# End of a decoder layer on TensorE: the rest of a row added by two matmuls, the last quarter squared from PSUM, and weight halves moved by 64 bytes

## The chip, the cores and the metric

One core of a Trainium2 chip runs the kernel. Its engines are TensorE (PE in the profile, with its weight loads as PEld), VectorE (DVE), ScalarE (ACT), GpSimd (POOL) and SyncE (SP, which issues most DMAs). Each engine works through its own queue in order and waits on semaphores for the others. The metric is the device time in microseconds (us); lower is better. For the kernel before it is 483.59 us, the median of three runs (483.5, 483.85 and 483.59).

## The reference

One layer of a hybrid decoder for 256 tokens of width 1024, cut to what matters here:

```
mix = hybrid_mixer(x, ...)                       # mLSTM branch + attention branch, gated, projected
x   = layer_norm(ALPHA * x + mix, ln1_g, ln1_b)
u   = causal_dwconv(x @ w_up, conv_ffn)          # 1024 -> 2 * 2816, three taps along the tokens
g, up = split(u)
ffn = (silu(g) * up) @ w_down                    # 2816 -> 1024
x   = layer_norm(ALPHA * x + ffn, ln2_g, ln2_b)  # mean and variance over the 1024 columns of a token
```

Everything is float32. The kernel keeps that precision by splitting each operand of a product into a high part and a low part of type fp32r and adding three products: high with high, high with low, low with high.

## The kernel before

The weights stream through the core as 81 chunks of 128 rows x 2048 columns (1 MB each); `chunk_order` writes their order out by hand. SP loads a chunk into `raw` five steps ahead; two steps ahead ACT rounds it to the high part `wh` (a CAST) and DVE subtracts to get the low part `wl`. `mm3` issues the three products of one tile. For each chunk a step function (`step_up`, `step_dn`, ...) issues PE's work; `elem_work`, called ahead of it, issues the evacuation of the chunk before and the pieces of the split, in the order of a hand-written list in which `None` stands for the next piece of the split.

The end of the layer. `up` chunks make the hidden features: chunk `up i` gives 128 of them for all 256 tokens; ACT and DVE take them from PSUM (`up_evac`), apply the convolution and the gate, and split the result into `hh` and `hl` (two tiles of 128 x 256; columns 0 to 127 are tokens 0 to 127). `dn` chunks are `w_down`: chunk `dn d` holds the rows for features 2d and 2d+1, each row 1024 columns wide. The last chunks come in the order up 20, up 21, dn 8, dn 9, dn 10, so the three last `dn` chunks (numbers 78, 79 and 80 in the order, with hidden tiles 16 to 21) are worked on together. For up 20 and up 21 and the chunk before them ACT also sums the rows of the weight chunks (`row_sums`), so that a row of the product can give its own mean.

The output is 256 tokens x 1024 columns. Token half 0 accumulates in the PSUM tiles `ffn00` and `ffn01` (columns 0 to 511 and 512 to 1023). Token half 1 has `ffn10`, `ffn11`; for the three last chunks its second 512 columns are dealt with as two quarters, the last 256 columns plus two columns of sums in `ffn11` and columns 512 to 767 in `self.quarter` (`ffn12`). What half 1 had gathered before the last three chunks is added to ALPHA times the input in a tile `r` in SBUF by `so_far`, many microseconds earlier.

PE's order in the last stage is: token half 0 (36 matmuls of 512 columns), token half 1's first 512 columns (18 of 512), then 18 of 258 columns, then 18 of 256 columns into `ffn12`. In `finish`, DVE adds `ffn12` to `r` less the mean (L1201), ACT squares that (L1202), ACT takes the square root of the variance (L1204), DVE the reciprocal (L1205), and three DVE multiplications (L1207) with three stores end the program.

Where the halves of a weight row lie is set by `shift`, `odd` and `col`. In the last three chunks before the change, every 512-column half begins 224 bytes into a stretch of 256 bytes of SBUF (by the addresses in the built program), and so does each `hh` and `hl` tile. In the `up` products the moving operand (`x1h`, `x1l`) begins at 64 of 256 and the stationary weights at 128.

Of the kernel before, what the change touches and what calls it, by code (L numbers as in the profile page):

```python
# [11 lines left out]
F32R = mybir.dt.float32r  # L12
BF16 = mybir.dt.bfloat16
AF = mybir.ActivationFunctionType
ALU = mybir.AluOpType
# [3 lines left out]
P = 128  # L19
S = 256  # L20
D = 1024
# [3 lines left out]
NF = D_FF // P  # L25
# [7 lines left out]
WCOLS = KT * 264 + 64  # L33
# [27 lines left out]
def shift(kind, i):  # L61

    if kind in ("vm", "vb", "o"):
        return 48
    if kind in ("wa", "wb"):
        return 56
    if kind == "dn":

        return 40
    return 0 if kind == "wo" else 16  # L70


class Kernel:
# [27 lines left out]
    def split_parts(self, s):  # L101
        if s >= len(self.order) or s in self.w:
            return []
        raw = self.raw.pop(s)
        if s in self.extra:
            wh, wl = self.extra.pop(s)
            a = 8
        else:
            wh = self.stream.tile([P, WCOLS], F32R, tag="wh", name=f"wh{s}", bufs=3)
            wl = self.stream.tile([P, WCOLS], F32R, tag="wl", name=f"wl{s}", bufs=3)  # L110
            a = shift(*self.order[s])

        e, z, n, _ = odd(*self.order[s])
        last = self.order[s][0] == "dn" and self.order[s][1] >= NF // 2 - 3
        wh, wl = (t[:, a - e:a + 2048 + z + 2 * last] for t in (wh, wl))
        edges = sorted({0, 256 if e else 0, 512 if s == 4 else 0, 2048 if self.order[s][0] == "up" and self.order[s][1] >= 6 else 1024, 2048 - n, 2048})
        cuts = [(*(t[:, self.col(s, b):self.col(s, b) + d - b] for t in (wh, wl)), raw[:, b:d])
                for b, d in zip(edges, edges[1:])]
        self.w[s] = (wh, wl)
        if last:  # L120
            self.summed[self.order[s][1] - (NF // 2 - 3)] = s, raw
        return [lambda c=c: self.split_into(*c) for c in cuts]

    def row_sums(self, n):
# [5 lines left out]

    def split_sums(self, n):
        s, _ = self.summed.pop(n)
        a = self.col(s, D)
        wh, wl = (bass.AP(t.tensor, t.offset + D, [list(t.ap[0]), [a, 2], [1, 2]]) for t in self.w[s])
        self.split_into(wh, wl, self.sums[:, n])

    def col(self, s, c):

        e, z, n, _ = odd(*self.order[s])
        return c + (e if c >= 256 else 0) + (z if c >= 2048 - n else 0)  # L140


# [962 lines left out]
    def step_dn(self, s, d, *a):  # L1105
        nc = self.nc
        if d == 0:
            self.st = [self.ln_tiles(f"2_{t}") for t in range(2)]
            a0 = [self.ps_side([P, 512], f"ffn0{h}") for h in range(2)]
            a1 = [self.ps_side([P, 512], f"ffn1{h}") for h in range(2)]  # L1110
            self.acc = [list(zip(a, ((0, 512), (512, 1024)))) for a in (a0, a1)]
            self.sums = self.fp.tile([P, 3, 2, 2], F32, name="sums")
            nc.gpsimd.memset(self.sums, 0.0)
            self.few = self.fp.tile([P, 8], F32, name="few")

            self.quarter = self.ps_side([P, 256], "ffn12")

        d0 = NF // 2 - 3

        def mm(dd, kk, t, ps, cols, fresh=0):  # L1120
            b = self.col(self.order.index(("dn", dd)), kk * D)
            w = [x[:, b + cols[0]:b + cols[1]] for x in self.w[self.order.index(("dn", dd))]]
            k = 2 * dd + kk
            hh, hl = (x[:, t * P:(t + 1) * P] for x in self.hid[k])
            self.mm3(ps, hh, hl, w[0], w[1], k == fresh, k == (2 * d0 if t and not fresh else NF) - 1)

        def part(t, q):
            ps, cols = self.acc[t][q]
            self.ln_part(self.st[t], self.x1[:, t, :], ps, cols)

        if d < d0:
            for kk in range(2):
                for t in range(2):
                    for ps, cols in self.acc[t]:
                        mm(d, kk, t, ps, cols)
            self.w.pop(s)
            if d == d0 - 1:
                r = self.st[1]["r"]

                def so_far(q):  # L1140
                    ps, cols = self.acc[1][q]
                    c = slice(*cols)
                    nc.vector.scalar_tensor_tensor(r[:, c], self.x1[:, 1, c], ALPHA, ps, op0=ALU.mult, op1=ALU.add)

                def total():
                    nc.scalar.activation(self.st[0]["r"], r, AF.Copy, accum_out=self.few[:, 0:1])
                self.evac[s] = [lambda: so_far(0), lambda: so_far(1), None, total]
            return

        ks = [(d0 + i, kk) for i in range(3) for kk in range(2)]  # L1150
        (p0, c0), (p1, c1) = self.acc[1]
        if d == d0:
            for k in ks:
                for q in self.acc[0]:
                    mm(*k, 0, *q)
            nc.scalar.activation(self.few[:, 7:8], self.mhalf[:, 0:1], AF.Sqrt, scale=-1.0)
            self.evac[s] = [lambda: part(0, 0), lambda: part(0, 1), lambda: self.ln_scale(self.st[0]),
                            lambda: self.ln2_out(0)]
        else:
            if d == d0 + 1:  # L1160
                for k in ks:
                    mm(*k, 1, p0, c0, 2 * d0)

                def add():
                    r = self.st[1]["r"][:, 0:512]
                    nc.vector.tensor_add(r, r, p0)
                self.evac[s] = [add]
            else:
                for k in ks:
                    mm(*k, 1, p1[:, 0:258], (768, D + 2), 2 * d0)  # L1170
                for k in ks:
                    mm(*k, 1, self.quarter, (512, 768), 2 * d0)

    def ln2_out(self, t):
        r = self.st[t]["r"]
# [7 lines left out]
    def finish(self):  # L1183

        nc, v, g, act = self.nc, self.nc.vector, self.nc.gpsimd, self.nc.scalar
        r, c = self.st[1]["r"], self.x1[:, 0, :]
        junk = self.fp.tile([P, 512], F32, name="junk")
        gain, bias = self.lnrow
        total, mean, s0, s1, base, sq, rs = (self.few[:, i:i + 1] for i in range(7))
        ps = self.acc[1][1][0]  # L1190
        lo, mid, hi = slice(0, 512), slice(512, 768), slice(768, D)
        v.tensor_scalar(mean, ps[:, 256:257], total, 1.0 / D, op0=ALU.add, op1=ALU.mult)
        act.activation(junk, r[:, lo], AF.Square, bias=mean, scale=-1.0, accum_out=s0)
        v.scalar_tensor_tensor(r[:, hi], ps[:, 0:256], mean, r[:, hi], op0=ALU.subtract, op1=ALU.add)
        act.activation(junk[:, 0:256], r[:, hi], AF.Square, scale=1.0 / 32.0, accum_out=s1)
        v.scalar_tensor_tensor(c[:, lo], r[:, lo], mean, gain[:, lo], op0=ALU.subtract, op1=ALU.mult)
        g.tensor_scalar(s0, s0, 1.0 / D, EPS, op0=ALU.mult, op1=ALU.add)
        v.tensor_mul(c[:, hi], r[:, hi], gain[:, hi])
        g.tensor_tensor(base, s0, s1, op=ALU.add)

        v.scalar_tensor_tensor(r[:, mid], self.quarter, mean, r[:, mid], op0=ALU.subtract, op1=ALU.add)  # L1201
        act.activation(junk[:, 0:256], r[:, mid], AF.Square, scale=1.0 / 32.0, accum_out=sq)  # L1202
        v.tensor_mul(c[:, mid], r[:, mid], gain[:, mid])
        act.activation(rs, sq, AF.Sqrt, bias=base)  # L1204
        v.reciprocal(rs, rs)  # L1205
        for q in (slice(0, 384), slice(384, 768), hi):
            v.scalar_tensor_tensor(c[:, q], c[:, q], rs, bias[:, q], op0=ALU.mult, op1=ALU.add)  # L1207
            self.store(1, c, q.start, q.stop)
# [7 lines left out]
def odd(kind, i):  # L1216

    if kind == "kb":
        return 0, 8, 128, False
    if kind == "ga" and i < NG - 1:  # L1220
        return 0, 8, 128, True
    if kind == "dn" and i >= NF // 2 - 3:
        return 0, 64, 1024, False
    if (kind, i) == ("up", 2):
        return 0, 8, 256, True
    if (kind, i) in (("up", 0), ("up", 1)):
        return 8, 0, 0, False
    return 0, 0, 0, False
# [14 lines left out]
def _layout(w_in, b_in, conv_qk, mlstm_norm, rel_bias, w_branch_a, w_branch_b, w_out, ln1_g, ln1_b, w_up, conv_ffn,  # L1243
# [22 lines left out]
    def col(a):  # L1266
        return a.reshape(-1, P).T

    vec = np.concatenate(
        [col(b_in[o:o + D]) for o in (O_QM, O_KM, O_QB, O_KB, O_VB, O_GA, O_GB)]  # L1270
        + [col(conv_qk), col(mlstm_norm), col(ln1_g), col(ln1_b), col(conv_ffn)], axis=1)
    rows = np.stack([b_in[O_O:O_O + D], b_in[O_VM:O_VM + D], ln1_g, ln1_b, ln2_g, ln2_b])
    dist = 255 - np.arange(LTOE)
# [33 lines left out]
```

## Time and profile before

| what | before |
|---|---|
| device time, median of 3 | 483.59 us |
| the profiled execution: from first to last instruction | 481.8 us |
| PE, share of the span | 473.9 us, 98% |
| DVE, ACT, POOL | 77%, 62%, 5% |
| mean granted TensorE clock | 0.995 |
| first matmul on the last three chunks | 458.38 us |
| end of the last matmul | 475.15 us |
| from there to the end of the span | 6.65 us |

The profile gives the profiled execution's time as its span; start and end around the span account for the other 1.8 us of the median, and are taken to be equal before and after. Times in the rows are counted from the start of the span. "A <- B" in a row reads "A is written from B". A row with an entry in square brackets had to wait, and the entry names whom for.

### The profile page before, as it was taken

How to read it: one execution, taken by the hardware profiler on the slowest of the kernel's cores; microseconds unless marked ns; L12 is line 12 of the kernel's file. 1: busy time of each engine (PE TensorE's matmuls, PEld its weight loads, DVE VectorE, ACT ScalarE, POOL GpSimd, SP SyncE). 2: the span in 40 equal slices, each digit the busy share in tenths (PEclk: the TensorE clock that was granted, in tenths of full speed). 3: DMA queues.
4: the chain of work that ended last, by engine and by line, in shares of the span. 5: the costliest groups of instructions: out<-in, count | busy, mean ns of one | idle time of the engine just before them, and what ended most of it. 6: DMA issues, size and time to landing. Idle time of an engine off the chain costs nothing.

```text
span 481.8 us, 9426 instructions
## 1 busy us (share of the span) xinstructions
PE 473.9 (98%) x3831; PEld 459.0 (95%) x3831; DVE 370.9 (77%) x666; ACT 298.6 (62%) x509; POOL 22.4 (5%) x42
## 2 busy tenths in 40 slices
PE   8999999999999999999999999999999999999994
PEld 6999999999999999999999999999999999999984
DVE  5798986887688668985677788878668766767886
ACT  6579676685758666966655623766456544655861
POOL 0301002000100010002000001000000000000000
PEclk9999999999999999999999999999999999999998
DMA  7995555464636463643954591727564655455202
GB/s 234 321 325 213 193 188 185 175 222 145 192 136 236 166 192 105 260 177 129 377 195 174 178 346 61 290 88 263 175 209 169 220 190 182 174 210 220 88 1 90
DMA packets 18988, 92.71 MB, mean 192 GB/s; under 512 B 2338, under 2 KB 5614, under 8 KB 9726
## 3 DMA queue, kind: packets, MB, share of 16 engines
q1 hardware_dynamic: 17710, 87.85, 50.8%
q0 software_dynamic: 1232, 4.24, 3.2%
q8 instruction: 30, 0.49, 0.4%
q14 instruction: 16, 0.12, 0.1%
HBM read 91.02 MB, written 1.06 MB: 191 GB/s over the span
## 4 chain that ended last, share of the span: by engine, by line
PE 98%; DVE 0%; ACT 0%; issue 0%; DVEq 0%; ACTq 0%
PE ps_up L148 25%; PE ffn L148 13%; PE ps_ga L148 5%; PE ps_kb L148 5%; PE ps_gb L148 5%; PE ps_qb L148 5%; PE ps_qm L148 5%; PE ps_vm L148 5%; PE mix L148 5%; PE ps_vb L148 5%; PE ps_wb L148 5%; PE ps_wa L148 5%; PE ps_km L148 5%; PE ps_o0b L434 1%; PE ps_o0a L434 1%; PE psn L148 1%
## 5 line engine op out<-in xcount | busy, mean ns | idle before, releaser
L95 DVE TENSOR_TENSOR wl<-raw,wh 128x1024 fp32r<-128x1024 f32 (+4 forms) x147 | 180.0, 1262 | 26.2 <-ACT wh L94 23.5
L94 ACT CAST wh<-raw 128x1024 fp32r<-128x1024 f32 (+4 forms) x147 | 151.9, 1080 | 7.3 <-DMA raw<-in_wst_dram 4.1
L148 PE MATMUL ps_up<-x1h,wl 128*128 128x256 f32 x320 | 88.5, 276 | 0.0
L148 PE MATMUL ps_up<-x1h,wh 128*128 128x256 f32 x320 | 88.4, 276 | 0.0
L148 PE MATMUL ps_up<-x1l,wh 128*128 128x256 f32 x320 | 88.4, 276 | 0.0
L148 PEld LDWEIGHTS ps_up<-x1l,wh 128*128 128x128 f32 x320 | 60.1, 188 | 0.4
L148 PEld LDWEIGHTS ps_up<-x1h,wh 128*128 128x128 f32 x320 | 60.1, 188 | 0.3
L148 PEld LDWEIGHTS ps_up<-x1h,wl 128*128 128x128 f32 x320 | 60.1, 188 | 0.0
L1085 DVE SCALAR_TENSOR_TENSOR cu<-ps_up,vec,cu 128x255 f32<-128x255 f32 (+1 forms) x80 | 33.1, 476 | 20.4 <-ACT cu L1081 20.4
L148 PE MATMUL ffn<-wh,hl 128*128 128x512 f32 (+2 forms) x94 | 35.5, 378 | 0.0
L148 PE MATMUL ffn<-wl,hh 128*128 128x512 f32 (+2 forms) x94 | 35.5, 377 | 0.0
L148 PE MATMUL ffn<-wh,hh 128*128 128x512 f32 (+2 forms) x94 | 35.3, 375 | 0.0
L94 ACT CAST hh<-cu 128x256 fp32r<-128x256 f32 x22 | 8.9, 406 | 40.4 <-DVE cu L1096 40.4
L1081 ACT ACTIVATE cu<-ps_up,vec 128x256 f32<-128x256 f32 x40 | 16.7, 469 | 22.5 <-PE ps_up L148 22.5
L148 PEld LDWEIGHTS ffn<-wh,hl 128*128 128x128 f32 x94 | 17.7, 188 | 3.2
L148 PEld LDWEIGHTS ffn<-wl,hh 128*128 128x128 f32 x94 | 17.7, 188 | 3.1
L148 PEld LDWEIGHTS ffn<-wh,hh 128*128 128x128 f32 x94 | 17.7, 188 | 3.0
L148 PE MATMUL ps_ga<-xth,wh 128*128 128x256 f32 x64 | 18.0, 281 | 0.0
L148 PE MATMUL ps_qm<-xth,wh 128*128 128x256 f32 x64 | 17.9, 280 | 0.0
L148 PE MATMUL mix<-wh,mgh 128*128 128x256 f32 x64 | 17.8, 279 | 0.0
L148 PE MATMUL ps_qb<-xth,wh 128*128 128x256 f32 x64 | 17.8, 278 | 0.0
L148 PE MATMUL ps_gb<-xth,wh 128*128 128x256 f32 x64 | 17.8, 278 | 0.0
(340 smaller groups left out, 1445.0 us busy)
## 6 DMA issues: line engine op xcount, KB each, us to landing
raw<-in_wst_dram SPq DMA_DIRECT2D x72, 1024.0 KB, 4.9
raw<-in_wst_dram SPq DMA_DIRECT2D x10, 512.0 KB, 6.7
raw<-in_wst_dram SPq DMA_DIRECT2D x8, 256.0 KB, 4.5
lnrow<-in_rows_dram POOLq DMA_DIRECT2D x4, 512.0 KB, 6.7
xraw<-in_xt_dram SPq DMA_DIRECT2D x8, 128.0 KB, 2.8
toe<-table POOLq DMA_DIRECT2D x4, 256.0 KB, 5.3
xtok<-in_x_dram POOLq DMA_DIRECT2D x1, 1024.0 KB, 8.1
sgb<-in_wst_dram SPq DMA_DIRECT2D x4, 128.0 KB, 3.5
```

Of the source, the lines that this page charges most:

```text
L94: self.nc.scalar.copy(wh, raw)
L95: self.nc.vector.tensor_sub(wl, raw, wh.bitcast(F32))
L148: self.nc.tensor.matmul(ps, a[i], b[i], start=start and i == 0, stop=stop and i == 2)
L434: mm(ps[t], x[:, k, t * P:(t + 1) * P], w, start=start and k == 0, stop=stop and k == KT - 1)
L1081: act.activation(cu[:, j, :], ps[:, j, :], AF.Copy, scale=tap(2, j))
L1085: v.scalar_tensor_tensor(cu[:, j, o:], ps[:, j, :S - o], tap(t, j), cu[:, j, o:], op0=ALU.mult, op1=ALU.add)
```

## The change

Three things are edited.

1. In the three last `dn` chunks the second halves of the two rows lie elsewhere in `wh` and `wl`: they now begin 160 bytes into a stretch of 256 bytes, 64 lower than before; the first halves stay at 224. A split's piece is still one row of 1024 columns, but it is now written as two runs of 512.
2. Token half 0's second 512 columns are worked on as two pieces of 256. The loops are turned for that: all 18 matmuls of the first 512 columns come first, over all three chunks, then 36 matmuls of 256 columns.
3. The rest of the row (columns 512 to 767 of `r`) is split into high and low parts (`res`) after step dn 7, and two matmuls with an identity (`unit`) add it to `ffn12` ahead of the last quarter. `finish` then has ACT square `ffn12` out of PSUM, with the mean as a bias, and DVE apply the gain to `ffn12` directly; the two DVE instructions L1201 and L1203 become one (L1226), and a one-column multiplication (L1221) is new.

The diff, cut to its core (line numbers after it are higher by 13 to 23 than before):

```diff
     def split_parts(self, s):
...
+        if last:
+            wh, wl = (t[:, 0:WCOLS] for t in (wh, wl))
...
+            def halves(t, k):
+                b, c = self.col(s, k * D), self.col(s, k * D + 512)
+                return bass.AP(t.tensor, t.offset + b, [list(t.ap[0]), [c - b, 2], [1, 512]])
...
     def col(self, s, c):
+        if kind == "dn" and i >= NF // 2 - 3:
+            k, c = divmod(c, D)
+            return ((552, 1064) if c < 512 else (24 - 512, 1624 - 512))[k] + c
...
     def step_dn(self, s, d, *a):
...
+                def keep():
+                    nc.scalar.copy(self.unit, self.ident)
+                    self.split_into(*self.res, r[:, 512:768])
+                self.evac[s] = [lambda: so_far(0), lambda: so_far(1), None, total, keep]
...
         if d == d0:
+            (a0, b0), (a1, _) = self.acc[0]
             for k in ks:
-                for q in self.acc[0]:
-                    mm(*k, 0, *q)
+                mm(*k, 0, a0, b0)
+            for k in ks:
+                for j in range(2):
+                    mm(*k, 0, a1[:, j * 256:(j + 1) * 256], (512 + j * 256, 768 + j * 256), open=j == 0)
...
                 for k in ks:
                     mm(*k, 1, p1[:, 0:258], (768, D + 2), 2 * d0)
+                for i, h in enumerate(self.res):
+                    nc.tensor.matmul(self.quarter, self.unit, h, start=i == 0, stop=False)
                 for k in ks:
-                    mm(*k, 1, self.quarter, (512, 768), 2 * d0)
+                    mm(*k, 1, self.quarter, (512, 768), 2 * d0, True)
...
     def finish(self):
...
+        v.tensor_scalar(part, mean, 1.0 / 32.0, None, op0=ALU.mult)
         v.tensor_mul(c[:, hi], r[:, hi], gain[:, hi])
...
-        v.scalar_tensor_tensor(r[:, mid], self.quarter, mean, r[:, mid], op0=ALU.subtract, op1=ALU.add)
-        act.activation(junk[:, 0:256], r[:, mid], AF.Square, scale=1.0 / 32.0, accum_out=sq)
-        v.tensor_mul(c[:, mid], r[:, mid], gain[:, mid])
+        act.activation(junk[:, 0:256], self.quarter, AF.Square, bias=part, scale=-1.0 / 32.0, accum_out=sq)
+        v.scalar_tensor_tensor(c[:, mid], self.quarter, mean, gain[:, mid], op0=ALU.subtract, op1=ALU.mult)
```

What it does to the order of the instructions, at three places. In the rows a name's number tells the buffers of one kind apart: `hh18` is the hidden tile 18, `wh79` the high part of chunk 79.

PE before, the 13th to 18th matmul of the last stage (the first one stands just behind the last matmul of up 21): they work on hidden tile 18 and chunk 79, once for each half of the columns.

```order
L148 MATMUL ffn00_4129<-wh79_5539,hh18_5410 128x512
L148 MATMUL ffn00_4129<-wl79_5540,hh18_5410 128x512
L148 MATMUL ffn00_4129<-wh79_5539,hl18_5411 128x512
L148 MATMUL ffn01_4130<-wh79_5539,hh18_5410 128x512
L148 MATMUL ffn01_4130<-wl79_5540,hh18_5410 128x512
L148 MATMUL ffn01_4130<-wh79_5539,hl18_5411 128x512
```

PE after, the 13th to 20th matmul of the same stage.

```order
L161 MATMUL ffn00_4129<-wh80_5617,hh20_5558 128x512
L161 MATMUL ffn00_4129<-wl80_5618,hh20_5558 128x512
L161 MATMUL ffn00_4129<-wh80_5617,hl20_5559 128x512
L161 MATMUL ffn00_4129<-wh80_5617,hh21_5630 128x512
L161 MATMUL ffn00_4129<-wl80_5618,hh21_5630 128x512
L161 MATMUL ffn00_4129<-wh80_5617,hl21_5631 128x512
L161 MATMUL ffn01_4130<-wh78_5473,hh16_5244 128x256
L161 MATMUL ffn01_4130<-wl78_5474,hh16_5244 128x256
```

Chunk 80 and the hidden tiles 20 and 21 have moved up: the first use of `wl80` from the 26th matmul to the 14th, that of `hh21` from the 31st to the 16th, that of `hl21` from the 33rd to the 18th. What makes them, on ACT and DVE, has not moved.

ACT before, from the gate of up 21 to the end of the program:

```order
L1081 ACTIVATE cu_5613<-ps_up_5562,vec 128x256 x2
L94 CAST wh_5611<-raw_5416 128x1024 x2
L1092 ACTIVATE cu_5613<-cu_5613 128x256
L128 ACTIVATE r_0_4121,sums<-raw_5416 128x1024 x2
L94 CAST hh_5624<-cu_5613 128x256
L94 CAST wh_5611<-sums 128x2x2
L1156 ACT_TABLE_LOAD
L1156 ACTIVATE few<-mhalf 128x1
L1193 ACTIVATE junk,few<-r_1_4125,few 128x512
L1195 ACTIVATE junk,few<-r_1_4125 128x256
L1202 ACTIVATE junk,few<-r_1_4125 128x256
L1204 ACTIVATE few<-few 128x1
```

ACT after, the same place:

```order
L1094 ACTIVATE cu_5619<-ps_up_5568,vec 128x256 x2
L94 CAST wh_5617<-raw_5422 128x2x512 x2
L1105 ACTIVATE cu_5619<-cu_5619 128x256
L136 ACTIVATE r_0_4121,sums<-raw_5422 128x1024 x2
L94 CAST hh_5630<-cu_5619 128x256
L94 CAST wh_5617<-sums 128x2x2
L1177 ACT_TABLE_LOAD
L1177 ACTIVATE few<-mhalf 128x1
L1216 ACTIVATE junk,few<-r_1_4125,few 128x512
L1218 ACTIVATE junk,few<-r_1_4125 128x256
L1225 ACTIVATE junk,few<-ffn_4139,few 128x256
L1227 ACTIVATE few<-few 128x1
```

The order is the same: two casts of chunk 80 and two sums of its rows stand ahead of the cast of hidden tile 21. The casts write two runs of 512 each, and the last square reads `ffn12` (here `ffn_4139`).

DVE at the end, before:

```order
L1198 TENSOR_TENSOR x_3016<-r_1_4125,lnrow_4303 128x256
L1201 SCALAR_TENSOR_TENSOR r_1_4125<-ffn_4136,few,r_1_4125 128x256
L1203 TENSOR_TENSOR x_3016<-r_1_4125,lnrow_4303 128x256
L1205 RECIPROCAL few<-few 128x1
L1207 SCALAR_TENSOR_TENSOR x_3016<-x_3016,few,lnrow_4305 128x384 x2
L1207 SCALAR_TENSOR_TENSOR x_3016<-x_3016,few,lnrow_4305 128x256
```

And after:

```order
L1221 TENSOR_SCALAR few<-few 128x1
L1222 TENSOR_TENSOR x_3016<-r_1_4125,lnrow_4306 128x256
L1226 SCALAR_TENSOR_TENSOR x_3016<-ffn_4139,few,lnrow_4306 128x256
L1228 RECIPROCAL few<-few 128x1
L1230 SCALAR_TENSOR_TENSOR x_3016<-x_3016,few,lnrow_4308 128x384 x2
L1230 SCALAR_TENSOR_TENSOR x_3016<-x_3016,few,lnrow_4308 128x256
```

One instruction fewer stands between the last matmul and the reciprocal; L1226 waits for ACT's square (L1225), where L1201 waited for PE. The orders of SP and POOL are the same in both kernels.

More of the change, by code (lines that the diff above doesn't have):

```diff
@@ L114, in split_parts @@
         last = self.order[s][0] == "dn" and self.order[s][1] >= NF // 2 - 3
-        wh, wl = (t[:, a - e:a + 2048 + z + 2 * last] for t in (wh, wl))
+        if last:
+            wh, wl = (t[:, 0:WCOLS] for t in (wh, wl))
+            self.w[s] = (wh, wl)
+            self.summed[self.order[s][1] - (NF // 2 - 3)] = s, raw
+            def halves(t, k):
+                b, c = self.col(s, k * D), self.col(s, k * D + 512)
+                return bass.AP(t.tensor, t.offset + b, [list(t.ap[0]), [c - b, 2], [1, 512]])
+            return [lambda k=k: self.split_into(halves(wh, k), halves(wl, k), raw[:, k * D:(k + 1) * D].rearrange(
+                "p (a b) -> p a b", a=2)) for k in range(2)]
+        wh, wl = (t[:, a - e:a + 2048 + z] for t in (wh, wl))
         edges = sorted({0, 256 if e else 0, 512 if s == 4 else 0, 2048 if self.order[s][0] == "up" and self.order[s][1] >= 6 else 1024, 2048 - n, 2048})
@@ L119, in split_parts @@
         self.w[s] = (wh, wl)
-        if last:
-            self.summed[self.order[s][1] - (NF // 2 - 3)] = s, raw
         return [lambda c=c: self.split_into(*c) for c in cuts]
@@ L132, in split_sums @@
         s, _ = self.summed.pop(n)
-        a = self.col(s, D)
-        wh, wl = (bass.AP(t.tensor, t.offset + D, [list(t.ap[0]), [a, 2], [1, 2]]) for t in self.w[s])
+        a, b = (self.col(s, k * D + 512) + 512 for k in range(2))
+        wh, wl = (bass.AP(t.tensor, t.offset + a, [list(t.ap[0]), [b - a, 2], [1, 2]]) for t in self.w[s])
         self.split_into(wh, wl, self.sums[:, n])
     def col(self, s, c):
-        e, z, n, _ = odd(*self.order[s])
+        kind, i = self.order[s]
+        if kind == "dn" and i >= NF // 2 - 3:
+            k, c = divmod(c, D)
+            return ((552, 1064) if c < 512 else (24 - 512, 1624 - 512))[k] + c
+        e, z, n, _ = odd(kind, i)
         return c + (e if c >= 256 else 0) + (z if c >= 2048 - n else 0)
@@ L1114, in step_dn, with mm @@
             self.few = self.fp.tile([P, 8], F32, name="few")
+            self.unit = self.fp.tile([P, P], F32R, name="unit")
+            self.res = [self.fp.tile([P, 256], F32R, name=f"res{n}") for n in "hl"]
             self.quarter = self.ps_side([P, 256], "ffn12")
         d0 = NF // 2 - 3
-        def mm(dd, kk, t, ps, cols, fresh=0):
-            b = self.col(self.order.index(("dn", dd)), kk * D)
-            w = [x[:, b + cols[0]:b + cols[1]] for x in self.w[self.order.index(("dn", dd))]]
+        def mm(dd, kk, t, ps, cols, fresh=0, more=False, open=False):
+            b = self.col(self.order.index(("dn", dd)), kk * D + cols[0])
+            w = [x[:, b:b + cols[1] - cols[0]] for x in self.w[self.order.index(("dn", dd))]]
             k = 2 * dd + kk
             hh, hl = (x[:, t * P:(t + 1) * P] for x in self.hid[k])
-            self.mm3(ps, hh, hl, w[0], w[1], k == fresh, k == (2 * d0 if t and not fresh else NF) - 1)
+            self.mm3(ps, hh, hl, w[0], w[1], k == fresh and not more, k == (2 * d0 if t and not fresh else NF) - 1 and not open)
         def part(t, q):
@@ L1146, in total @@
                     nc.scalar.activation(self.st[0]["r"], r, AF.Copy, accum_out=self.few[:, 0:1])
-                self.evac[s] = [lambda: so_far(0), lambda: so_far(1), None, total]
+                def keep():
+                    nc.scalar.copy(self.unit, self.ident)
+                    self.split_into(*self.res, r[:, 512:768])
+                self.evac[s] = [lambda: so_far(0), lambda: so_far(1), None, total, keep]
             return
@@ L1188, in finish @@
         gain, bias = self.lnrow
-        total, mean, s0, s1, base, sq, rs = (self.few[:, i:i + 1] for i in range(7))
+        total, mean, s0, s1, base, sq, rs, part = (self.few[:, i:i + 1] for i in range(8))
         ps = self.acc[1][1][0]
@@ L1221, in odd @@
         return 0, 8, 128, True
-    if kind == "dn" and i >= NF // 2 - 3:
-        return 0, 64, 1024, False
     if (kind, i) == ("up", 2):
```

## The prediction

> **What bounds the kernel now.** I read the page's chain first, then the end of the chain of waits, then the rows of ACT, DVE and PE in the last stage.
>
> ```profile
> PE 473.9 (98%) x3831; PEld 459.0 (95%) x3831; DVE 370.9 (77%) x666; ACT 298.6 (62%) x509; POOL 22.4 (5%) x42
> ```
>
> PE is busy for 98% of the span, so the time is PE's matmuls plus what stands behind the last one. The chain of waits from 454.9 us (start, length, what):
>
> ```profile
> 454.91 3.63 PE ps_up L148 x32
> 458.55 16.61 PE ffn L148 x90
> 475.15 0.03 issue
> 475.18 0.49 DVE r L1201
> ...
> 475.71 0.34 issue
> 476.05 0.52 ACT junk L1202 x2
> ...
> 476.65 0.30 ACT few L1204
> ...
> 476.98 0.17 DVE few L1205
> ```
>
> PE runs through the last stage without a gap, and 1.83 us pass from its end (475.15) to the reciprocal (476.98). The change works on both. So I ask first whether PE still has its operands in time. ACT and DVE in that stage (start, length):
>
> ```profile
> 459.03 0.83 ACT L1081 ACTIVATE cu<-ps_up,vec 128x256 f32<-128x256 f32 x2
> 459.75 1.99 ACT L94 CAST wh<-raw 128x1024 fp32r<-128x1024 f32 x2
> 461.96 1.05 ACT L128 ACTIVATE r<-raw 128x1024 f32<-128x1024 f32 x1
> 463.13 1.06 ACT L128 ACTIVATE r<-raw 128x1024 f32<-128x1024 f32 x1
> 464.19 0.40 ACT L94 CAST hh<-cu 128x256 fp32r<-128x256 f32 x1
> ...
> 461.46 2.35 DVE L95 TENSOR_TENSOR wl<-raw,wh 128x1024 fp32r<-128x1024 f32 x2
> 463.73 0.42 DVE L1096 TENSOR_TENSOR cu<-cu 128x256 f32<-128x256 f32 x1
> 464.62 0.43 DVE L95 TENSOR_TENSOR hl<-cu,hh 128x256 fp32r<-128x256 f32 x1 [0.47 <-ACT hh L94]
> ```
>
> These make chunk 80 and hidden tile 21. The first row of `wl80` is done at about 462.65 (half of 2.35 behind 461.46), `hh21` at 464.59, `hl21` at 465.05. PE's 1st, 13th, 14th, 19th, 31st and 33rd matmul of the stage:
>
> ```profile
> 458.38 0.39 PE L148 MATMUL ffn<-wh,hh 128*128 128x512 f32 x1
> ...
> 461.14 0.39 PE L148 MATMUL ffn<-wh,hh 128*128 128x512 f32 x1
> 461.37 0.39 PE L148 MATMUL ffn<-wl,hh 128*128 128x512 f32 x1
> ...
> 462.50 0.39 PE L148 MATMUL ffn<-wh,hh 128*128 128x512 f32 x1
> ...
> 465.23 0.39 PE L148 MATMUL ffn<-wh,hh 128*128 128x512 f32 x1
> ...
> 465.68 0.39 PE L148 MATMUL ffn<-wh,hl 128*128 128x512 f32 x1
> ```
>
> One per 0.227 us (4.54 us for 20). Before, the 31st is the first to use `hh21` and starts 0.64 us after it is there; the 33rd has 0.63 us to spare for `hl21`. That is all the slack there is.
>
> **The turned loops.** By the order, `wl80` is now wanted by the 14th matmul, `hh21` by the 16th and `hl21` by the 18th, while their makers stay where they are: up 21 ends on PE at 458.5 as before, and ACT is full from then to the cast of `hh21`. What a weight load costs that PE could not take ahead shows at 82.5 us, where one waited:
>
> ```profile
> 82.52 0.19 PEld L822 LDWEIGHTS pso<-pth,vbh 128*128 128x128 f32 x1
> 82.55 0.36 PE L822 MATMUL pso<-pth,vbh 128*128 128x256 f32 x1
> ...
> 82.75 0.38 PE L823 MATMUL pso<-ptf,vbf 128*128 128x128 f32 x2
> ```
>
> A 256-column matmul is followed after 0.20 us there instead of 0.11, so 0.09 a time. Then: 14th due at 461.37, waits for 462.65, starts at about 462.73; 15th at 463.05 (0.227 + 0.09); 16th due at 463.28, waits for 464.59, starts at 464.65; 17th at 464.97; 18th at 465.20, when `hl21` is just there; the next begins at 465.43. Before, the 19th begins at 462.50. The first wait is 1.3 us, the second 1.3 to 1.4, and the stage stands **2.93 us later**. Nothing covers it: PE's queue is in order, and the 36 quarter matmuls that could run meanwhile are queued behind the waiting ones. Bounds: without any cost of loads 2.75, with a third exposed load 3.05.
>
> **The pieces of 256 and the 64 bytes.** The rate of a 256-column matmul differs by place:
>
> ```profile
> 470.67 0.28 PE L148 MATMUL ffn<-wh,hh 128*128 128x258 f32 x1
> ...
> 472.82 0.28 PE L148 MATMUL ffn<-wh,hh 128*128 128x256 f32 x1
> ...
> 474.86 0.28 PE L148 MATMUL ffn<-wh,hl 128*128 128x256 f32 x1
> ```
>
> The 18 of 258 columns take 2.15 us (0.119 each) and the last 18 follow each other in 0.120, while `ps_up` in the chain does 32 in 3.63, 0.1134 each. In `ps_up` the weights loaded next lie 64 bytes further on (modulo 256) than the moving operand; in the last stage both lie at 224. The change makes it 160 and 224, the same 64, so I take 0.1134 (0.1143 for 258 columns). Then token half 0's 36 pieces cost 4.08 us against 18 x 0.227 = 4.09: nothing. The 18 of 258 gain 0.09, the last 17 spacings 0.11. If 0.120 stays: 0, 0 and +0.24 for the pieces, so 0.44 worse together. [...] This trace has both rates side by side, so I go by the rows.
>
> **The two added matmuls.** `res` and `unit` lie both at 64 of 256, a distance that no fast group has: 0.12 each, **+0.24** (bounds 0.23 at the fast rate, 0.41 with both loads exposed). Their making, in `keep`, is two ACT casts of at most 0.41 us and one DVE subtraction of 0.43, after step dn 7. The cover is there:
>
> ```profile
> 442.25 0.84 ACT L1081 ACTIVATE cu<-ps_up,vec 128x256 f32<-128x256 f32 x2 [2.15 <-PE ps_up L148]
> ...
> 443.13 1.66 DVE L1085 SCALAR_TENSOR_TENSOR cu<-ps_up,vec,cu 128x255 f32<-128x255 f32 x4 [1.74 <-ACT cu L1081]
> ```
>
> ACT sat idle 2.15 us and DVE 1.74 before the evacuation that follows, so it costs nothing; without that cover at most 0.8 us, and up 18's gate would be late for dn 9, ten microseconds on. The casts and subtractions in two runs of 512 have no row of their own; I take the 1024 row, give 0.1 us either way, and it enters through `wl80` and `hh21`.
>
> PE's end: +2.93 - 0.09 + 0.24 - 0.11 = **+2.97**, at about 478.1.
>
> **Token half 0's normalisation** is DVE's work beside PE:
>
> ```profile
> 467.44 0.67 DVE L975 SCALAR_TENSOR_TENSOR r<-x,ffn 128x512 f32<-128x512 f32 x1
> ...
> 472.51 0.68 DVE L1166 TENSOR_TENSOR r<-r,ffn 128x512 f32<-128x512 f32 x1
> ```
>
> From its second half to the end of L1166 it needs 5.75 us. `ffn01` is now done at about 469.7, so DVE is free at 475.5; the mean (L1215) is due when the 258-column matmuls end, at about 475.8. Hidden by 0.3 us; if that goes, the excess is added only as far as it passes the 2.3 us of PE behind it.
>
> **The tail.** Before: 1.83 us from PE's end to the reciprocal. After: ACT waits for PE in the semaphore instruction that held L1202 back, so I keep the 0.34 us of issue seen ahead of it: the square starts 0.39 after PE's end. It took 0.52 from SBUF; from PSUM I add 0.05:
>
> ```profile
> L1081 ACT ACTIVATE cu<-ps_up,vec 128x256 f32<-128x256 f32 x40 | 16.7, 469 | 22.5 <-PE ps_up L148 22.5
> ```
>
> (469 ns for 256 columns from PSUM against 0.42 from SBUF), so it ends at 0.96. L1226 may not touch `ffn12` before that: 0.98 to 1.47 (0.49 as L1201). The root ends at 1.35. The reciprocal follows at 1.47 instead of 1.83: **-0.36**. If the 0.34 of issue is not met again, -0.70; if the square is no shorter and DVE starts late, -0.2. Behind the reciprocal nothing changes.
>
> **The sum:** +2.97 - 0.36 = +2.61 on a span of 481.8, 484.4; the median is 1.8 above the span, so 483.59 + 2.61 = **486.2 us** (+0.54%). With the ends of every term together: 485.5 to 486.9.
>
> **Rivals.**
> A. *The clock falls during the waits.* Rows of the granted clock (PEclk ahead of the DMA share) behind PE's end:
>
> ```profile
> 476.00:477.00 1.00, 0.00 (x0) 0.00 (x0) 0.14 (x2) 0.80 (x3) 0.00 (x0) 1.00 0.03 8
> 477.00:478.00 1.00, 0.00 (x0) 0.00 (x0) 0.96 (x3) 0.00 (x0) 0.00 (x0) 0.53 0.00 0
> ```
>
> It fell to 0.5 at 477.06, after 1.9 us without a matmul. The two waits together are 2.7 us with 0.5 us of matmuls between. Against it: neither alone is 1.9. How long the half rate would last is bounded from above by the start of the kernel:
>
> ```profile
> 1.25 3.60 PE L202 MATMUL warm_ps<-warm 128*128 128x512 bf16 x8 [1.25 <-DVE warm L199]
> ...
> 6.09 0.28 PE L434 MATMUL ps_o3b<-wh,xth 128*128 128x264 f32 x1
> ```
>
> Full rate came 4.8 us after the first matmul, so a fall costs 0 to 2.4 us; I take 1.5: 487.7. [...]
>
> B. *The 64 bytes do nothing* (the change doesn't do what it says): 486.2 + 0.44 = 486.6.
>
> C. *No slower: the wait is short.* If the two-run casts and subtractions of chunk 80 ran much faster, `hh21` would come earlier. Without any wait the rest sums to -0.09 + 0.24 - 0.11 - 0.36 = -0.32: 483.3. For the time to stay within 0.2% (0.97 us, about what a measurement of this kernel can tell from no change) the delay must fall from 2.93 to under 1.29, so chunk 80's casts (1.99 us) would have to shrink to some 0.35 and the subtractions (2.35) likewise. For it speaks only that no row shows the two-run form; against it, that the number of elements is the same.
>
> **Chances.** The forecast 0.57, A 0.28, B 0.08, C 0.05, something else that makes it faster 0.02. The likeliest is 486.2. The range reaches from the low end of the forecast, 485.5, over B to 488.0, which leaves out the dear end of A: about 0.15 lies outside. Slower by over 0.2%: 0.93; within: 0.05; faster: 0.02, since without any wait the tail alone gives 0.3 to 0.7 us.
>
> **What would show it.** In the trace after: two gaps on PE at 461.4 to 462.7 and 463.3 to 464.6, the second ended by ACT's `hh` cast; `ffn` matmuls of 256 columns at 0.1134; PE's last end near 478.1; L1225 0.39 us after it, the reciprocal 1.47 after it; granted clock 1.0 until then, or 0.5 in a row near 464 to 468 (A). I am wrong if PE shows no gap there, or if it takes the pieces of 256 columns first.

## The result, and the profile after

The changed kernel takes **487.75 us**, the median of six runs (485.82, 487.62, 487.68, 487.82, 487.91, 490.05), against 483.74 for the kernel before in six runs beside it: a ratio of **1.0081 (95% interval 1.0069 to 1.0094)**. It is slower, as forecast, and 1.55 us slower than the likeliest case said. Four of the six stand within 0.3 us of each other, at the 487.7 of rival A. Of 21 executions of the kernel before beside the first four experiments one took 975.13 us; the ratios there leave it out.

The profiled execution took 487.62 with a span of 485.9 us, 4.1 more than before. First line 1 of the page, then the timeline of PE at the start of the last stage (start, length, and in brackets the idle time ahead and what ended it).

```profile
PE 475.9 (98%) x3851; PEld 460.8 (95%) x3851; DVE 370.5 (76%) x667; ACT 299.1 (62%) x511; POOL 22.4 (5%) x42
```

```profile
458.51 0.39 PE L161 MATMUL ffn<-wh,hh 128*128 128x512 f32 x1
...
461.27 0.39 PE L161 MATMUL ffn<-wh,hh 128*128 128x512 f32 x1
462.86 0.50 PE L161 MATMUL ffn<-wl,hh 128*128 128x512 f32 x1 [1.20 <-DVE wl L95]
463.20 0.40 PE L161 MATMUL ffn<-wh,hl 128*128 128x512 f32 x1
464.76 0.50 PE L161 MATMUL ffn<-wh,hh 128*128 128x512 f32 x1 [1.17 <-ACT hh L94]
...
465.56 0.28 PE L161 MATMUL ffn<-wh,hh 128*128 128x256 f32 x1
```

The two gaps are where the prediction put them, and the tiles it named end them. PE's share of the span still reads 98%: 2.4 us of idle time do not show in a share. What follows shows in the table by stretches. Its columns are the stretch, its length, the busy time of PE, PEld, DVE, ACT and POOL with their instructions, then the granted clock, the DMA share and GB/s.

```profile
458.89:462.31 3.42, 2.77 (x13) 1.91 (x11) 2.79 (x7) 3.42 (x8) 0.00 (x0) 1.00 0.00 0
462.31:465.72 3.41, 1.69 (x7) 1.05 (x8) 2.46 (x5) 3.36 (x7) 0.00 (x0) 1.00 0.00 0
465.72:469.13 3.41, 3.41 (x19) 3.41 (x18) 1.38 (x2) 0.59 (x2) 0.00 (x0) 0.50 0.02 5
...
465.56:471.28 5.72, 5.72 (x38) 5.71 (x36) 1.38 (x2) 0.75 (x2) 0.00 (x0) 0.70 0.01 3
471.28:475.37 4.09, 4.09 (x20) 3.38 (x19) 3.72 (x9) 0.00 (x0) 0.68 (x1) 1.00 0.01 2
475.37:477.55 2.18, 2.18 (x19) 2.17 (x18) 1.88 (x5) 0.00 (x0) 0.00 (x0) 1.00 0.33 126
```

From 465.72 to 469.13 the clock is 0.50. PE is full there and does half the work: 256-column matmuls follow each other every 0.213 us, instead of 0.11 behind 469.22. The 36 pieces take the 5.72 us of the fourth row, where 18 matmuls of 512 columns take 4.09 (18 x 0.227). The end, from the chain of waits:

```profile
464.76 12.95 PE ffn L161 x75
477.71 0.23 PE ffn L1193 x2
477.95 2.05 PE ffn L161 x18
480.00 0.03 ACTq L1225
480.03 0.05 issue
480.07 0.57 ACT junk L1225 x2
...
480.67 0.48 DVE x L1226
481.16 0.08 DVE few L1228
...
481.26 0.62 DVE x L1230
```

Before, the first of the last multiplications stood here in the chain:

```profile
477.17 0.62 DVE x L1207
```

From PE's end to it, it is 1.26 us now (480.00 to 481.26); before it was 2.02 (475.15 to 477.17). So PE's end is 4.85 us later, and the tail gives 0.76 back: 4.1 us of span.

### The profile page after: what moved, and what is told of

It reads as the page before. It is cut to its first block, busy times and chain, and to the rows that moved or that the text cites. A ratio compares the mean times of both kernels' runs of the same rounds, so it can differ in the third digit from the quotient of the medians.

```text
span 485.9 us, 9470 instructions
## 1 busy us (share of the span) xinstructions
PE 475.9 (98%) x3851; PEld 460.8 (95%) x3851; DVE 370.5 (76%) x667; ACT 299.1 (62%) x511; POOL 22.4 (5%) x42
## 4 chain that ended last, share of the span: by engine, by line
PE 93%; ACT 4%; issue 1%; DMA 1%; DVE 0%; SPq 0%; DVEq 0%; ACTq 0%
PE ps_up L161 21%; PE ffn L161 12%; PE ps_ga L161 5%; PE ps_kb L161 4%; PE ps_gb L161 4%; PE ps_qb L161 4%; PE ps_qm L161 4%; PE ps_vm L161 4%; PE mix L161 4%; PE ps_vb L161 4%; PE ps_wb L161 4%; PE ps_wa L161 4%; PE ps_km L161 4%; ACT wh L94 1%; ACT r L136 1%; PE ps_o0a L447 1%
## 5 line engine op out<-in xcount | busy, mean ns | idle before, releaser
L161 PE MATMUL ffn<-wl,hh 128*128 128x512 f32 (+2 forms) x100 | 37.3, 373 | 1.2 <-DVE wl L95 1.2
L161 PE MATMUL ffn<-wh,hh 128*128 128x512 f32 (+2 forms) x100 | 37.0, 370 | 1.2 <-ACT hh L94 1.2
L161 PE MATMUL ffn<-wh,hl 128*128 128x512 f32 (+2 forms) x100 | 37.2, 372 | 0.0
L161 PEld LDWEIGHTS ffn<-wh,hh 128*128 128x128 f32 x100 | 19.6, 196 | 4.3 <-ACT hh L94 1.6
L161 PEld LDWEIGHTS ffn<-wl,hh 128*128 128x128 f32 x100 | 19.5, 195 | 4.4 <-DVE wl L95 1.6
L161 PEld LDWEIGHTS ffn<-wh,hl 128*128 128x128 f32 x100 | 19.6, 196 | 3.1 <-DVE hl L95 0.2
```

What stands on the lines that cost most here:

```text
L161: self.nc.tensor.matmul(ps, a[i], b[i], start=start and i == 0, stop=stop and i == 2)
```

## The experiments

Times are medians of runs beside the kernel before, in about the order in which they were run. Each heading names the kernel that the edit is against; "ratio" is always to the kernel before.

**The turned loops turned back** (against the changed kernel; eleven runs). The split layout, the pieces, the added matmuls and the new tail stay; only the order over rows is that of before.

```
                 mm(*k, 0, a0, b0)
-            for k in ks:
                 for j in range(2):
```

> The changed kernel with one thing undone: token half 0 goes chunk row by chunk row again (first 512 columns, then the two pieces of 256, then the next row), so that chunk 80 and hidden tile 21 are wanted late, as before. Theory W (the turned loops make PE wait, and the waits make the clock fall): no gap on PE over 0.3 us in the last stage, granted clock 1.0 until PE's end, and what is left of the change counts: tail -0.76 (1.07 us from PE's end to the reciprocal, as the changed kernel's trace has it, against 1.83), the two added matmuls +0.24, the last 18 matmuls at 0.1134 -0.11, 258 columns +0.02: -0.6 us against before, about 483.1. Rival P (the pieces of 256 or the moved halves themselves slow PE or bring the clock down): still slower than before by 1.5 us or more, with the half rate somewhere in the pieces.

Measured: 483.31 against 483.75, ratio **0.9988 (0.9979 to 0.9997)**. No gap on PE, clock 1.00 up to PE's end. Its end, from the chain of waits:

```profile
473.64 2.05 PE ffn L161 x18
475.70 0.03 ACTq L1224
475.73 0.05 issue
475.77 0.57 ACT junk L1224 x2
...
476.37 0.48 DVE x L1225
...
476.96 0.62 DVE x L1229
```

The tail is 1.26 us, as in the changed kernel. All of the loss is the order of the loops; what is left of the change is a gain of some 0.4 us. It is a little smaller than the tail's 0.76 because PE's stage (from its first matmul to its last end) is 17.04 us instead of 16.75.

**Idle matmuls in both waits** (against the changed kernel; four runs). Six matmuls of 512 columns into an unused PSUM tile stand ahead of each row of chunk 80, so that PE has work while it would wait.

```
             for k in ks:
+                if k[0] == d0 + 2:
+                    filler(6)
                 mm(*k, 0, a0, b0)
```

> The changed kernel with matmuls of no use in the waits: ahead of each of chunk 80's two rows in the turned loop six 512-column matmuls of ready operands go into a PSUM tile that nobody reads (1.36 us each time, about the length of the wait). Theory W with the clock as a second step: chunk 80's operands come no earlier, so the last matmul ends as late as in the changed kernel without a fall of the clock (its one run without one was 485.82), granted clock 1.0 through the stage: 485.8 to 486.1. Rival (the clock does not follow PE's idleness, or the 1.7 us has another cause, such as the pieces of 256): 487.6 or more, the 256-column matmuls at 0.21 us for some 3.4 us as in the changed kernel.

Measured: 486.22 (485.84 to 486.32), ratio 1.0045 (1.003 to 1.006), clock 1.00 up to PE's end. From the chain of waits:

```profile
461.45 1.36 PE idle L1178 x6
462.81 0.79 PE ffn L161 x3
463.60 1.38 PE idle L1178 x6
```

The two waits are still there, as 2.74 us of idle matmuls, and the stage takes 20.04 us: 3.00 more than with the loops turned back. Without the gaps' effect on the clock the time is 1.5 us below the changed kernel's, and it is the prediction's likeliest case, 486.2, to the tenth. That close an agreement is luck: the stage is 3.29 us longer than before where +2.97 was forecast, and the tail 0.76 shorter where 0.36 was. So the loss has two parts: 2.9 to 3.0 us of waits and about 1.5 us of clock.

**The turned loops alone** (against the kernel before; four runs). One matmul for the second 512 columns, old layout, old tail.

```
-            for k in ks:
-                for q in self.acc[0]:
+            for q in self.acc[0]:
+                for k in ks:
                     mm(*k, 0, *q)
```

> The kernel before with only the two loops of token half 0 turned: all 18 matmuls of its first 512 columns, then 18 of 512 columns for the second; halves, tail and last quarter as before. Theory W: both waits are there (1.2 to 1.4 us each at the 14th and 16th matmul), +2.8 us, and the clock falls in most runs, +1.7: 486.5 where it doesn't fall, 488.2 where it does, median near 488. Rival P: the loops alone cost little, under 1 us, 483.7 to 484.7.

Measured: 487.49 (486.67 to 488.41), ratio 1.0074 (1.0059 to 1.0088). PE, and the end in the chain of waits:

```profile
463.00 0.50 PE L148 MATMUL ffn<-wl,hh 128*128 128x512 f32 x1 [1.20 <-DVE wl L95]
...
464.91 0.50 PE L148 MATMUL ffn<-wh,hh 128*128 128x512 f32 x1 [1.17 <-ACT hh L94]
```

```profile
480.57 0.32 issue
480.89 0.52 ACT junk L1202 x2
```

The same two gaps, the same half clock behind them (0.50 from 465.72 to 469.13 in this execution), the stage 4.59 us longer than before. In the stretch ahead of the fall PE was busy for 1.55 us:

```profile
462.30:465.72 3.42, 1.55 (x6) 0.90 (x7) 2.62 (x5) 3.37 (x8) 0.00 (x0) 1.00 0.00 0
```

The pieces of 256 columns and their layout have no part in the loss. The median is no higher than the changed kernel's although the old tail is 0.76 us longer; the four executions lie 1.7 us apart (486.67, 487.02, 487.97, 488.41), so the clock probably did not cost the same in each; only the slowest of them has a trace.

**The tail alone** (against the kernel before; eleven runs). `res`, `unit`, their two matmuls and the new lines of `finish`; loops and layout as before.

```
+                for i, h in enumerate(self.res):
+                    nc.tensor.matmul(self.quarter, self.unit, h, start=i == 0, stop=False)
                 for k in ks:
-                    mm(*k, 1, self.quarter, (512, 768), 2 * d0)
+                    mm(*k, 1, self.quarter, (512, 768), 2 * d0, True)
...
-        act.activation(junk[:, 0:256], r[:, mid], AF.Square, scale=1.0 / 32.0, accum_out=sq)
+        act.activation(junk[:, 0:256], self.quarter, AF.Square, bias=part, scale=-1.0 / 32.0, accum_out=sq)
```

> The kernel before with only the tail of the change: the rest of the row added by two matmuls with the identity, ACT squares the last quarter from PSUM; halves and loops as before. If the tail is worth what the changed kernel's trace shows (1.07 us instead of 1.83 from PE's end to the reciprocal) and the two matmuls cost 0.24: -0.5 us, about 483.2. If the 0.34 us of issue ahead of the square comes back: 1.4 to 1.5 us and -0.15. If splitting the rest of the row delays the up stage: no gain, 483.7 or more.

Measured: 483.32 (482.96 to 483.71), ratio **0.9988 (0.998 to 0.9997)**. From the chain of waits:

```profile
473.11 0.23 PE ffn L1177 x2
473.34 2.16 PE ffn L148 x18
475.50 0.03 ACTq L1209
475.53 0.05 issue
475.57 0.57 ACT junk L1209 x2
```

The whole gain comes from this part. The last 18 matmuls take 2.16 us here and 2.05 where their operand lies 64 bytes lower.

**The second half in one matmul** (against the first experiment; eleven runs): no pieces of 256 columns for token half 0.

```
-                for j in range(2):
-                    mm(*k, 0, a1[:, j * 256:(j + 1) * 256], (512 + j * 256, 768 + j * 256), open=j == 0)
+                mm(*k, 0, a1, b1)
```

> The first experiment's kernel (loops interleaved, halves moved, new tail) with token half 0's second 512 columns worked on in one matmul again instead of two pieces of 256. In the first experiment the pieces cost 0.1175 us each, 4.23 us for 36, where 18 matmuls of 512 columns at 0.227 cost 4.09. If a 512-column matmul from the moved halves keeps 0.227: 0.15 us less than the first experiment, 483.15. If the moved halves suit 256 columns only, and 512 go at 0.233 to 0.237 as some rows at the start of the stage: within 0.05 us of it, 483.3.

Measured: 483.58 (483.13 to 484.36) against 483.91, ratio 0.9994 (0.9985 to 1.0003). The stage is 17.07 us, with the pieces 17.04. One matmul of 512 or two of 256 make no difference that can be seen here.

**The square's bias from a tile** (against the kernel before; one run). The issue time ahead of the square had shrunk from 0.34 to 0.05 us, which the prediction had only as a bound of its sum. The changed kernel's square has a bias column; here the old square gets one, of zeros.

```
-        act.activation(junk[:, 0:256], r[:, mid], AF.Square, scale=1.0 / 32.0, accum_out=sq)
+        act.activation(junk[:, 0:256], r[:, mid], AF.Square, bias=self.zero[:, 0:1], scale=1.0 / 32.0, accum_out=sq)
```

> The kernel before; the last square (L1202) is given a bias column of zeros from a tile, as the changed kernel's square has a bias column. It tells why 0.34 us of issue stood ahead of the square before and 0.05 in the changed kernel. If the bias from a tile is the difference: about 0.05 us from the release to the square, and some 0.3 us less from PE's end to the reciprocal. If not (what runs beside it on DVE, or where it reads): 0.32 to 0.34 again.

Measured: 484.13 against 483.91. From the chain of waits:

```profile
476.20 0.34 issue
476.54 0.61 ACT junk L1204 x2
```

The 0.34 us stay; the bias is not their reason.

**Other distances** (against the first experiment; one run). The second halves of chunk 78, of chunk 79 and of chunk 80's two rows lie 96, 160, 32 and 0 bytes below the next weights (modulo 256), where the change has 64 for all.

```
-            return ((552, 1064) if c < 512 else (24 - 512, 1624 - 512))[k] + c
+            off = {0: (-8, -8), 1: (-24, -24), 2: (8, 16)}[i - (NF // 2 - 3)][k]
+            return ((552, 1064) if c < 512 else (24 - 512 + off, 1624 - 512 + off))[k] + c
```

> The first experiment's kernel with the second halves of the last three chunks' rows at other places: the weights loaded next (the hidden tiles, at 224 of 256 bytes) lie 96 bytes further on than the moving operand for chunk 78, 160 for chunk 79, 32 for the first row of chunk 80 and 0 for its second, instead of 64 for all. One look at the spacing of the last 18 matmuls (256 columns), six or three for each distance. If the distance sets the rate and 64 is its best: 0.120 at 0, as before the change, and more than 0.1134 at the others. If any place but the old one is as good: 0.1134 at 32, 96 and 160. If the place is not what matters: 0.1134 throughout.

Measured: 483.63 against 483.91. The last 18 matmuls, which go through all three chunks, from the chain of waits:

```profile
473.84 2.15 PE ffn L162 x18
```

At the four places together they take 2.15 us (0.118 to 0.119 from one to the next on the mean of each place), where at 64 bytes it was 2.05 in the first experiment (0.1133). With all at 0 bytes, in the tail alone, it was 2.16. So the place did act on these 18, and of the five distances only 64 did it. The edit moves the halves and the distance together, so it does not tell these two apart; in `ps_up`, where the halves lie elsewhere at the same 64 bytes, the rate is 0.1134 too.

**Idle matmuls in the first wait only** (against the changed kernel; four runs): the filler of the second experiment, only where the first row of chunk 80 begins.

```
+                if k == (d0 + 2, 0):
+                    filler(6)
                 mm(*k, 0, a0, b0)
```

> The changed kernel with matmuls of no use in the first of the two waits alone (six of 512 columns, 1.36 us), so that one wait of some 1.2 to 1.5 us is left at the 16th matmul. Theory: the clock falls when a window of some 3.4 us is idle for more than half; one wait is too short for that: granted clock 1.0 through the stage and 486.0 to 486.3 in every run, as with both waits filled. Rival: any wait over a microsecond can bring it down: some runs at 487.6 to 487.9.

Measured: 486.31 (486.17 to 486.52), ratio 1.005 (1.0036 to 1.0064). By stretches of 3.41 us:

```profile
462.36:465.77 3.41, 2.23 (x10) 1.31 (x9) 2.74 (x5) 3.36 (x8) 0.00 (x0) 1.00 0.00 0
465.77:469.18 3.41, 3.41 (x30) 3.37 (x29) 1.38 (x2) 0.87 (x2) 0.00 (x0) 1.00 0.02 5
```

One wait of 1.2 us alone leaves the clock at 1.00, at nearly the same place in time as in the changed kernel; it takes both. That points to a count over a stretch rather than to the length of a gap. Rows of the kernel before and of the one with the bias tile, behind PE's end, say how much is enough:

```profile
473.65:477.06 3.41, 1.49 (x13) 1.28 (x11) 2.18 (x6) 1.83 (x7) 0.47 (x2) 1.00 0.17 64
477.06:480.47 3.41, 0.00 (x0) 0.00 (x0) 1.62 (x4) 0.00 (x0) 0.00 (x0) 0.50 0.43 154
```

```profile
473.90:477.31 3.41, 1.70 (x15) 1.50 (x13) 2.31 (x5) 1.93 (x7) 0.47 (x2) 1.00 0.22 82
477.31:480.72 3.41, 0.00 (x0) 0.00 (x0) 1.71 (x4) 0.22 (x1) 0.00 (x0) 1.00 0.42 151
```

The stretches are laid back from where the clock changed. Behind 1.49 us of PE work it was halved; behind 1.70 it stayed, and fell one stretch later. With 1.69 in the changed kernel it fell. In the kernel before the trace has the clock full from 6.02 to 477.06, 138 times 3.413 us; in the changed kernel it was full from 4.92 to 465.72, 135 times, half to 469.13, once, and full to 482.79, four times. The border, between 1.69 and 1.70 us, is at about half of a stretch. On such stretches all thirteen profiles agree. Of those at full clock, nine with 0.04 to 1.69 us of PE work and six with none were each followed by the half clock, and none with 1.70 or more was.

**Two idle matmuls in each wait** (against the changed kernel; four runs) tests that border: PE idles some 0.7 us twice and keeps over half of any stretch.

```
+                if k[0] == d0 + 2:
+                    filler(2)
                 mm(*k, 0, a0, b0)
```

> The changed kernel with two idle matmuls of 512 columns (0.227 us each) ahead of each row of chunk 80 in the turned loop, where the earlier run had six. The waits still end when wl80 and hh21 are there, so PE's work behind them stays 2.9 us late. Theory 1: the clock is judged over windows of 3.41 us, and is halved behind a window in which PE was busy for no more than half (1.69 us and less in the windows seen so far; 1.70 and more left it at full). The two waits leave PE some 2.4 us without work in the changed kernel, and 1.5 us here, so every window of 3.41 us keeps at least 1.9 us of work wherever it lies: the clock stays at 1.0, and every execution takes 485.8 to 486.5 us. Theory 2: any pair of waits of about 0.8 us close together brings the clock down: 487.7 in most executions, as for the changed kernel. Theory 3: only the length of a single gap counts, and 1.3 us is just over it in some executions; here the gaps are 0.8 us, and it gives the same as theory 1.

Measured: 485.84 (485.59 to 486.21), ratio 1.0047 (1.003 to 1.0063), clock 1.00:

```profile
462.51:465.93 3.42, 2.73 (x14) 1.98 (x15) 2.42 (x5) 3.33 (x8) 0.00 (x0) 1.00 0.00 0
465.93:469.34 3.41, 3.41 (x32) 3.41 (x31) 0.79 (x2) 0.00 (x0) 0.00 (x0) 1.00 0.02 5
```

Two gaps of 0.75 and 0.69 us (ahead of the matmuls at 462.43 and 464.34) did not bring the clock down, so it isn't pairs of waits as such. It fits the border at half and does not prove it: by this experiment alone the length of the gaps could count too. But one gap of 1.2 us left the clock alone in the experiment before, and two brought it down, which the length of a gap does not explain.

**The gain's multiplication later** (against the kernel before; one run): DVE's second reading of `r` is moved away from the square.

```
-        v.tensor_mul(c[:, mid], r[:, mid], gain[:, mid])
         act.activation(rs, sq, AF.Sqrt, bias=base)
         v.reciprocal(rs, rs)
+        v.tensor_mul(c[:, mid], r[:, mid], gain[:, mid])
```

> The kernel before, with DVE's multiplication of the last quarter by the gain (L1203), which reads the same r as ACT's square, moved behind the reciprocal. In the kernel before ACT's square stands 0.34 us of issue behind the instruction that waited for DVE; in the changed kernel it stands 0.05 us behind. A bias column taken from a tile, as the changed kernel has one, left the 0.34 as it was. Theory 1: a second reader of r starting on DVE at the same moment held the square back; then it follows after about 0.05 us here, and the reciprocal comes 0.3 us sooner behind PE's end (1.5 us instead of 1.83). Theory 2: the 0.34 us belongs to being released by DVE's write instead of by PE; then it stays at 0.32 to 0.34 us. The time moves by less than 0.4 us either way: 483.4 to 484.2.

Measured: 483.71 against 483.70. From the chain of waits:

```profile
475.67 0.34 issue
476.01 0.52 ACT junk L1202 x2
```

**The square from PSUM, still behind DVE** (against the kernel before; one run): L1201 writes back into `ffn12`.

```
-        v.scalar_tensor_tensor(r[:, mid], self.quarter, mean, r[:, mid], op0=ALU.subtract, op1=ALU.add)
-        act.activation(junk[:, 0:256], r[:, mid], AF.Square, scale=1.0 / 32.0, accum_out=sq)
-        v.tensor_mul(c[:, mid], r[:, mid], gain[:, mid])
+        v.scalar_tensor_tensor(self.quarter, self.quarter, mean, r[:, mid], op0=ALU.subtract, op1=ALU.add)
+        act.activation(junk[:, 0:256], self.quarter, AF.Square, scale=1.0 / 32.0, accum_out=sq)
+        v.tensor_mul(c[:, mid], self.quarter, gain[:, mid])
```

> The kernel before, with L1201 writing its result back into ffn12 in PSUM instead of into r in SBUF; ACT squares it and DVE multiplies it by the gain from there. The release of the square still comes from DVE, but the source is PSUM, as in the changed kernel. The 0.34 us of issue ahead of the square stood as they were with a bias from a tile, and with the multiplication moved away. Theory 1: they come with a release by DVE; then they stay at 0.32 to 0.34. Theory 2: they come with a source in SBUF that was just written; then the square follows after 0.05 here, as in the changed kernel. Time by theory 1 483.3 to 484.1, by theory 2 some 0.2 less.

Measured: 483.84 against 483.85.

```profile
476.03 0.34 issue
476.37 0.48 ACT junk L1202 x2
```

Neither the bias nor a second reader nor the memory of the source is the reason of the 0.34 us. Two differences are left: the engine that releases the square (PE instead of DVE), and that ACT's semaphore instruction ahead of it then waits for two engines and ends with PE (479.24 to 480.03 in the changed kernel). Neither is the reason by itself, by rows of the kernel before. There ACT's first square is released by DVE too, and it starts 0.03 us behind DVE's end (473.33); its wait is its own, without a semaphore instruction ahead:

```profile
473.11 0.22 DVE L1192 TENSOR_SCALAR few<-ffn,few 128x1 f32<-128x1 f32 x1
473.36 0.72 ACT L1193 ACTIVATE junk<-r,few 128x512 f32<-128x512 f32 x1 [7.15 <-DVE few L1192]
```

And the root (L1204), whose semaphore instruction waits for one engine alone, ACT itself, stands 0.04 us of issue behind it (476.60). What remains possible is a semaphore instruction released by DVE; no run shows it apart from this one square.

## Why the prediction was right or wrong

The direction and the mechanism of the waits were right, and the time lies in the range given, which had been drawn up to 488.0 to take in most of rival A. The likeliest case, 485.5 to 486.9, was not what happened. Step by step, in the profiled execution:

- **The waits: right.** From the stage's first matmul to the first piece it is 7.05 us (458.51 to 465.56) against 4.12 before (458.38 to 462.50): +2.93, as forecast. `wl80` and `hh21` were late by what ACT's and DVE's rows of before said. A weight load that waited cost 0.11 us (0.34 from one matmul to the next, 462.86 to 463.20, instead of 0.23), where 0.09 was taken; the upper bound with a third such load is 3.02 by the prediction's own terms, not 3.05.
- **The clock: here the likeliest case failed.** It took the clock for safe because neither wait alone is 1.9 us, the time without a matmul that had gone ahead of the fall in the kernel before. The rule read from that row was wrong: what had gone ahead was a stretch with 1.49 of 3.41 us of work, and the two waits, with 0.7 us of PE work between them (462.86 to 463.59), leave 1.69. Rival A (0.28) is what came, and its price is that of the 36 pieces: 5.72 us instead of 4.09, 1.63 against the 1.5 taken; by the whole stage it is 1.45 against the run with idle matmuls in both waits (21.49 instead of 20.04), and between the medians of the two kernels 1.53. In the changed kernel the half clock lasted 3.41 us (465.72 to 469.13). A stretch of that length with 1.69 us of work went ahead of it; with the loops alone turned it was 1.55, in the kernel before 1.49.
- **The 64 bytes: half right.** The last 18 went from 0.120 to 0.1133 (2.05 against 2.16 with the new tail and the old layout): the forecast's -0.11. The 18 matmuls of 258 columns did not follow: 2.18 us against 2.15, where -0.09 was forecast. Why two more columns matter is open. The pieces of token half 0 follow each other in 0.113 us in the run with two idle matmuls a wait and in 0.118 in the run with six in the first wait, with the same operands in the same order. So 64 bytes alone do not fix the rate; what else does is open too.
- **The two added matmuls: right**, 0.24 (477.55 to 477.79), and the making of `res` and `unit` left no trace on PE.
- **Token half 0's normalisation: right.** DVE was ready 0.50 us ahead of the 258-column matmuls' end; 0.3 was forecast.
- **The tail: mis-sized.** -0.76 instead of -0.36, and beyond the -0.70 given as its bound. The step was to carry the 0.34 us of issue over to a square released by PE; it is 0.05 there. That is 0.3 of the difference. The other 0.1 is the reciprocal: it overlaps the end of L1226 (0.08 us in the chain behind it), where 0.17 had been counted from that end on.

The sum on PE: +2.93 for the waits, +1.63 for the clock, +0.03, +0.24 and -0.11 make +4.72; PE ends 4.85 later, and 0.13 of that stood there already when the stage began. Less the tail's 0.76 that is the 4.1 of the span. Forecast were +2.97 and -0.36: the errors (1.63 of clock, 0.12 of the 258-column matmuls, 0.13 ahead of the stage, and 0.4 of tail the other way) go in part against each other.

Rival C is excluded by the waits' length. Rival B is excluded by the last 18.

Open: the run of 485.82, with a span of 484.1 us, is where the kernel with idle matmuls in both waits is (484.1 to 484.6), so probably its stretches of 3.41 us lay so that the waits were shared out between two; which runs fell, only the profiled ones show. For the run of 490.05, 2.2 us above the four, there is no reason shown.

The versions that beat both kernels are the new tail alone (483.32) and the whole change with the rows in the old order (483.31), each with a ratio of 0.9988; the first has the smaller edit.

## What to carry to other kernels

Before an order of loops is turned, set each operand's first use against the end of its maker: PE's share of busy time, 98%, hid that the slack was 0.6 us in a stretch where the new order needed 2.9. Count short waits of PE together, over stretches of 3.4 us laid wherever they are worst: here two of 1.2 us left 1.69 us of work in one such stretch and cost another 1.5 us by the clock, and a few idle matmuls in them saved that. Releasing ACT straight from PE took a DVE instruction of 0.5 us off the end and, in this kernel, saved 0.3 us of issue time besides.

## What the runs showed of the hardware that was not expected

- In these profiles the clock was halved behind a stretch of 3.41 us in which PE was busy for 1.69 us or less (1.49, 1.55, 1.69), and stayed behind 1.70 and more (1.70, 2.23, 2.73). The ends of matmuls in the profile are modelled, so the border is "about half", no closer. In the changed kernel the half clock lasted one stretch, 465.72 to 469.13, and PE was full in it.
- ACT's last square stood 0.32 to 0.34 us of issue behind a release by DVE (five kernels), and 0.05 us behind one by PE (three kernels). It isn't every release by DVE: the first square stood 0.03 us behind one (473.33 to 473.36). The reason is open.
- The last 18 matmuls, of 256 columns, followed each other in 0.1133 us where the next weights lay 64 bytes further on (modulo 256) than the moving operand, and in 0.118 to 0.120 at 0, 32, 96 and 160 bytes. Token half 0's pieces, at 64 bytes, ran at either rate (0.113, 0.118). The rows of the last 18 differ by 5% (2.05 us against 2.15 and 2.16); why is not shown.
